# Eight products of a joint weight in float32 on the raw tiles, in place of 24 on split parts

## The chip, the core and the metric

The kernel runs on one core of one Trainium2 chip. The metric is the device time of one execution in microseconds. A core has a matrix engine (TensorE, PE in the profile, with its weight loads as PEld), a vector engine (VectorE, DVE), a scalar engine (ScalarE, ACT), GpSimd (POOL) and a sync engine (SyncE, SP) that issues most transfers. PE writes its products into PSUM, eight banks of 128 x 512 float32 values; the other engines read them from there. Each engine takes its instructions in order and waits for others by semaphores.

## The reference

One layer over 2048 positions of width 1024: a pooling branch and a gated recurrence, merged by gates and projected, and then a feed-forward part with a short convolution. What matters here is the pooling branch:

```python
mixed = jnp.einsum('bsgc,gcd->bsgd', pooled, pool_w).reshape(B, S, POOL_WIDTH)
return mixed * pool_scale
...
ya = pool_mixer(u_pool, pool_w[l], pool_scale[l]) @ w_pa[l]
...
merged = gates[:, :, 0] * ya + gates[:, :, 1] * yb
```

Two linear maps follow one another without anything between them: the mix of each group of 128 channels (pool_w, 4 groups of 128 x 128, with a scale for each channel), and w_pa (512 x 1024). The kernel multiplies the two weights with each other once, into a joint weight, and later applies that to the pooled channels.

## The kernel before

The 2048 positions are worked in blocks of 512, two blocks at a time (b0 = 0, then b0 = 2). For each pair come the input projection, the mixer with the recurrence, the branch projections, the output projection and the feed-forward part.

**Seven products for eight.** Each projection is written as a scheme of seven block products P1 to P7 (in the order P1, P6, P5, P7, P2, P4, P3 for the units of the input projection). A `Unit` has three PSUM banks, X, Z and V. P6 goes into Z, then P5 into V, then P7 into Z again. Between P6 and P7 DVE has to read Z out (`u2`, L1226 in the kernel before); between P7 and P4 it has to read it again (`u3`, L1230). So P7 can't start until `u2` is done. The trace calls both `u`.

**Split operands.** Nearly every product is made of three: each float32 operand is split into a high and a low part of type float32r, and high x high, high x low and low x high are added up in PSUM. A `Stream` prepares the weights: it loads a raw tile of 128 x 512 (`raw`, L198, on SP's queue, 8 buffers), ACT casts it to the high part (L232), DVE subtracts that from the raw tile (L233), and the pair is a tile `ops` (6 buffers). For some tiles POOL first adds two or more raw tiles (L461), and the sums are stored for the second pair of blocks (the `kw` tiles, L343).

**The order.** The program is written down once, with no loop on the chip. Each product of `mm` counts, and every six of them make a tick. A tick converts at most one weight (not more than `LOOKAHEAD` = 4 ahead of its use) and moves the waiting tasks on. The tasks are generators that wait some ticks between their steps: the recurrence of each head (`hgrn_task`, with small float32 products `pl`, `pk`, `pv`, `po` and `pt` on PE and long chains on DVE), the pooling sums, and the preparation of later weights. A scheduler then orders the instructions of each engine by a timeline of its own. So how many products a place has also decides where everything after it lands.

**The joint weight.** In the first pair of blocks, `both` runs after each of eight units of the input projection (from the unit `u`, 0 on). Its operand `pw` is the pooling weight: ACT scales it by the channel scale in four pieces (L409), and it is then split like every weight. The other operand, `cw`, is an eighth of w_pa, also split. Three products into a bank (`cw0` to `cw7` in the program, `cw` in the trace), a copy by ACT (L973) and two stores (`wb`, L979) finish one. The joint weight is read back as `pa` weights much later.

In the trace the units are fr (the recurrence's forget gate and query), gr (gates), ur (pooling channels) and pa; the number that follows in the program (gr0_2 is the gate unit 2 of the first pair) is left out there. All products made through `mm` show as L149.

Of the kernel before, what the change touches and what calls it, by code (L numbers as in the profile page):

```python
# [11 lines left out]
F32 = mybir.dt.float32  # L12
F32R = mybir.dt.float32r
U8 = mybir.dt.uint8
AF = mybir.ActivationFunctionType
# [3 lines left out]
P = 128  # L19
# [58 lines left out]
LOOKAHEAD = 4  # L78
# [4 lines left out]
def tile_trunk(  # L83
# [16 lines left out]
    pe, act, dve, pool, sp = nc.tensor, nc.scalar, nc.vector, nc.gpsimd, nc.sync  # L100
# [4 lines left out]
    opsp = ctx.enter_context(tc.tile_pool(name="opsp", bufs=N_OPS))  # L105
# [4 lines left out]
    def slot(name, cols=TB, dt=F32):  # L110
        return slots.tile([P, cols], dt, tag="s", name=name, padded_shape=[P, 528])
# [25 lines left out]
    def tick():  # L137
        stream.advance(1)
        for t in list(tasks):
            t.wait -= 1  # L140
            if t.wait <= 0 and t.live:
                t.step()
# [5 lines left out]
    def mm(*args, **kw):  # L148
        count[1] = pe.matmul(*args, **kw)  # L149
        count[0] += 1  # L150
        if count[0] % MM_PER_TICK == 0:
            tick()
# [16 lines left out]
    class Stream:  # L169
# [47 lines left out]
        def convert(self):  # L217
            j = len(self.tiles)
            key, fn, raws = self.ops[j]
            while any(r.tile is None for r in raws):  # L220
                self.load()
            for r in raws:
                r.add()
            store_kept()
            v = fn(f"w{j}")
            t = opsp.tile([P, 2, 512], F32R, tag="ops", name=f"ops{j}")
            n = int(np.prod(v.shape[1:]))
            hi, lo = t[:, 0, :n], t[:, 1, :n]
            if len(v.shape) == 3:
                hi = hi.rearrange("p (a b) -> p a b", a=v.shape[1])  # L230
                lo = lo.rearrange("p (a b) -> p a b", a=v.shape[1])
            self.mark = act.copy(hi, v)  # L232
            low = self.low = dve.tensor_tensor(lo, v, f32(hi), ALU.subtract)  # L233
            if j in self.pins:
                for ins, other in zip((self.mark, low), self.pins[j]):
                    behind(ins, other)
            self.tiles.append((key, t))
            self.load_ahead()
# [43 lines left out]
    stream = Stream()  # L282
# [57 lines left out]
    def store_kept():  # L340
        while keeping:
            d, t, later = keeping.pop(0)
            ins = sp.dma_start(d, t)  # L343
            if later:
                behind(ins, stream.low)

    def plan_one(key, src):
        r = stream.raw(src)
        stream.op(key, lambda nm, r=r: r.tile, [r])
# [51 lines left out]
            fn, raws = unit[p]()  # L401
            stream.op(key, fn, raws)

    def scaled_pool(r):
        def fn(nm):
            t = slot(f"{nm}p")
            for g in range(4):
                c = slice(g * P, (g + 1) * P)
                act.activation(t[:, c], r.tile[:, c], AF.Copy, scale=col(o_ps + g))  # L409
            return t  # L410
        return fn

    def plan_mixer(b0):
        plan_io(b0)
        for n, (kind, i) in enumerate(PROJ):
            if not b0 and (kind, i) == ("u", 0):
                r = stream.raw(pool_wt)
                stream.op("pw", scaled_pool(r), [r])
            plan_unit("in", w_in_t, kind, i, ORDER, b0)
            if not b0 and 0 <= n - CW_AT < 8:  # L420
                g, c = divmod(n - CW_AT, 2)
                plan_one("cw", w_pa[g][:, c * 512 : c * 512 + 512])
        for d in range(2):
            unit = weights_of_unit([(lambda d=d, q=q: w_both.get((d, q))) for q in range(4)])
            for p in ORDER:
                fn, raws = unit[p]()
                stream.op("pa", fn, raws)
        for i in range(8):
            plan_one("pb", w_pb_t[i // 2][:, i % 2 * 512 : i % 2 * 512 + 512])
        plan_rows("wo", w_o, R_OUT, KD // 2)  # L430
# [158 lines left out]
    o_n1, o_n2, o_bg, o_ps, o_lb, o_hg, o_cb, o_cw = offs  # L589
# [8 lines left out]
    def col(o):  # L598
        return cols[:, o : o + 1]
# [361 lines left out]
    def both(n, w_mix):  # L961
        g, c = divmod(n, 2)
        w = stream.get("cw")
        m = slice(g * P, (g + 1) * P)
        ps = bank(f"cw{n}")
        before = count[1]
        mm(ps, w_mix[:, 0, m], w[:, 0], start=True, stop=False)
        behind(count[1], before)
        mm(ps, w_mix[:, 0, m], w[:, 1], start=False, stop=False)
        mm(ps, w_mix[:, 1, m], w[:, 0], start=False, stop=True)  # L970
        stream.used(1)
        t = slot(f"cw{n}")
        act.copy(t, ps)  # L973
        q = 2 * c + g // 2
        for d in range(2):
            if (d, q) not in w_both:
                w_both[d, q] = dram.tile([P, 512], F32, tag=f"wb{d}{q}", name=f"wb{d}{q}")
            to = w_both[d, q].rearrange("p (e j m) -> p e j m", e=2, j=2)[:, :, g % 2]
            sp.dma_start(to, t[:, d * 256 : d * 256 + 256].rearrange("p (e m) -> p e m", e=2))  # L979
# [1016 lines left out]
```

## Time and profile before

| what | us |
|---|---|
| median of three runs (2512.33 to 2514.47) | 2512.68 |
| the profiled execution | 2511.63 |
| its span | 2509.9 |
| PE busy in the span | 2494.3 |
| DVE busy | 1997.0 |
| ACT busy | 1205.3 |
| POOL busy | 807.5 |
| first and last product of `cw` start at | 166.6 and 353.9 |

A line of a group gives the line of the code, the engine and operation, the output and inputs by the program's names, the shapes and the count, and then the busy time and the mean of one in ns. A line of a timeline begins with its start and its length in us; in brackets stands how long the engine was idle before it, and who released it. The chain of waits is read the same way, but each piece there is only the time that it adds to the chain. PE's products overlap, so the distance from start to start tells more than a product's own length. A float32 product shows in the trace as two records. "PEclk" is the share of TensorE's full clock that was granted.

### The profile page before, as it was taken

How to read it: one execution, taken by the hardware profiler on the slowest of the kernel's cores; microseconds unless marked ns; L12 is line 12 of the kernel's file. 1: busy time of each engine (PE TensorE's matmuls, PEld its weight loads, DVE VectorE, ACT ScalarE, POOL GpSimd, SP SyncE). 2: the span in 40 equal slices, each digit the busy share in tenths (PEclk: the TensorE clock that was granted, in tenths of full speed). 3: DMA queues.
4: the chain of work that ended last, by engine and by line, in shares of the span. 5: the costliest groups of instructions: out<-in, count | busy, mean ns of one | idle time of the engine just before them, and what ended most of it. 6: DMA issues, size and time to landing. Idle time of an engine off the chain costs nothing.

```text
span 2509.9 us, 35658 instructions
## 1 busy us (share of the span) xinstructions
PE 2494.3 (99%) x11436; PEld 2043.5 (81%) x11436; DVE 1997.0 (80%) x3519; ACT 1205.3 (48%) x2273; POOL 807.5 (32%) x1139
## 2 busy tenths in 40 slices
PE   9999999999999999999999999999999999999998
PEld 7887888888888888888888888887888888888887
DVE  7789778998998778885586777689979887778755
ACT  6534444434555445554554344443355555445534
POOL 4343354502354334451330201223033433325410
PEclk9999999999999999999999999999999999999999
DMA  8888788588898889897444343447444544447852
GB/s 272 270 206 231 233 219 258 203 243 249 203 260 230 231 226 241 265 363 246 126 148 151 117 130 107 139 147 255 130 150 122 154 149 139 150 135 247 320 165 100
DMA packets 257691, 497.68 MB, mean 198 GB/s; under 512 B 26912, under 2 KB 47520, under 8 KB 257184
## 3 DMA queue, kind: packets, MB, share of 16 engines
q1 hardware_dynamic: 189872, 317.53, 40.2%
q0 software_dynamic: 42656, 112.74, 17.8%
q10 hardware_dynamic: 24976, 65.13, 7.6%
q8 instruction: 90, 1.47, 0.2%
q14 instruction: 97, 0.79, 0.1%
HBM read 383.63 MB, written 189.27 MB: 228 GB/s over the span
## 4 chain that ended last, share of the span: by engine, by line
PE 90%; DVE 4%; ACT 1%; POOL 1%; DMA 1%; issue 1%; ACTq 0%; SPq 0%; POOLq 0%; DVEq 0%
PE dn_P L149 16%; PE up_Z L149 15%; PE up_V L149 10%; PE up_X L149 10%; PE wo_P L149 6%; PE gr_Z L149 4%; PE pb L149 4%; PE gr_V L149 3%; PE gr_X L149 3%; PE io_Z L149 3%; PE fr_Z L149 2%; PE io_V L149 2%; PE pl L1053 2%; PE ur_Z L149 1%; PE fr_V L149 1%; PE fr_X L149 1%
## 5 line engine op out<-in xcount | busy, mean ns | idle before, releaser
L232 ACT CAST ops<-raw 128x512 fp32r<-128x512 f32 x800 | 494.0, 621 | 860.9 <-PE dn_P L149 177.7
L233 DVE TENSOR_TENSOR ops<-raw,ops 128x512 fp32r<-128x512 f32 x800 | 596.6, 749 | 208.9 <-ACT ops L232 201.6
L1730 DVE SCALAR_TENSOR_TENSOR e<-h,cols,e 128x512 f32<-128x512 f32 x176 | 143.1, 817 | 31.3 <-ACT e L1728 26.7
L1728 ACT ACTIVATE e<-h,cols 128x512 f32<-128x512 f32 x176 | 142.2, 814 | 25.2 <-DVE h L1186 18.4
L988 POOL DMA_DIRECT2D g_P<-dg_P x154 | 84.3, 549 | 161.5 <-PE dn_P L149 110.9
L1733 DVE SCALAR_TENSOR_TENSOR e<-h,cols,e 128x512 f32<-128x512 f32 x176 | 133.8, 769 | 2.5
L1299 POOL TENSOR_TENSOR gf_P<-e,e 128x512 f32<-128x512 f32 x44 | 61.1, 1390 | 150.2 <-DVE e L1739 92.6
L461 POOL TENSOR_TENSOR raw<-raw,raw 128x512 f32<-128x512 f32 x36 | 50.4, 1401 | 167.5 <-DVE ops L233 115.6
L1299 POOL TENSOR_TENSOR gf_P<-gf_P,e 128x512 f32<-128x512 f32 x44 | 59.2, 1345 | 71.8 <-DVE e L1739 71.3
L1723 POOL COPY h<-h 128x2 f32<-128x2 f32 x88 | 40.5, 472 | 117.4 <-DVE h L1185 110.4
L1439 POOL TENSOR_TENSOR q<-q,qs 128x512 f32<-128x512 f32 x16 | 22.4, 1400 | 160.5 <-ACT qs L1438 160.5
L1725 POOL COPY hist<-h 128x2 f32<-128x2 f32 x88 | 36.2, 411 | 117.6 <-DVE h L1186 115.8
L1737 ACT ACTIVATE e<-e 128x512 f32<-128x512 f32 x88 | 55.6, 632 | 38.2 <-DVE e L1733 38.0
L1186 DVE TENSOR_TENSOR h<-up_u,up_V 128x512 f32<-128x512 f32 x88 | 60.0, 682 | 10.3 <-PE up_V L149 9.8
L1274 DVE TENSOR_TENSOR x<-x,wo_P 128x512 f32<-128x512 f32 x88 | 55.7, 679 | 7.7 <-PE wo_P L149 7.2
L1472 ACT ACTIVATE gt<-gt,cols 128x512 f32<-128x512 f32 x48 | 34.8, 726 | 56.0 <-DVE gt L1186 40.7
L1274 DVE TENSOR_TENSOR ac<-ac,dn_P 128x512 f32<-128x512 f32 x72 | 47.1, 680 | 16.5 <-PE dn_P L149 16.2
L1038 POOL COPY qm<-q 128x64 f32<-128x64 f32 x64 | 26.6, 448 | 103.4 <-DMA gd<-gt 20.0
L1753 POOL DMA_DIRECT2D dg_P<-gf_P x88 | 50.6, 576 | 8.1 <-POOL gf_P L1299 7.4
L1224 ACT COPY up_e<-up_X 128x512 f32<-128x512 f32 x44 | 25.8, 586 | 57.2 <-PE up_X L149 52.1
L1723 POOL COPY h<-hist 128x2 f32<-128x2 f32 x88 | 44.1, 508 | 27.7 <-DVE m_T42l L675 27.7
L1053 PE MATMUL pl<-qm,k 128*128 128x192 f32 x256 | 50.6, 328 | 0.0
(1337 smaller groups left out, 8077.7 us busy)
## 6 DMA issues: line engine op xcount, KB each, us to landing
g_P<-dg_P POOLq DMA_DIRECT2D x154, 256.0 KB, 6.1
raw<-in_w_up_t SPq DMA_DIRECT2D x132, 256.0 KB, 3.4
raw<-in_w_in_t SPq DMA_DIRECT2D x98, 256.0 KB, 3.6
dg_P<-gf_P POOLq DMA_DIRECT2D x88, 256.0 KB, 4.0
dg_P<-e SPq DMA_DIRECT2D x66, 256.0 KB, 3.4
raw<-in_w_dn SPq DMA_DIRECT2D x66, 256.0 KB, 4.2
x<-in_x SPq DMA_DIRECT2D x64, 256.0 KB, 5.0
gd<-gt ACTq DMA_DIRECT2D x64, 256.0 KB, 3.7
```

Of the source, the lines that this page charges most:

```text
L149: count[1] = pe.matmul(*args, **kw)
L232: self.mark = act.copy(hi, v)
L233: low = self.low = dve.tensor_tensor(lo, v, f32(hi), ALU.subtract)
L988: eng.dma_start(t, d)
L1053: ins = pe.matmul(pa_[:, c * 192 : c * 192 + 192], ks[:, (i + c) * P : (i + c + 1) * P], mv[:, c].rearrange("p s x -> p (s x)"), start=Tru ...
L1186: return dve.tensor_tensor(dst, t, ps, ALU.add if how == "add" else ALU.subtract)
L1274: dve.tensor_tensor(t, t, ps[j], ALU.add if sg > 0 else ALU.subtract)
L1299: pin(eng.tensor_tensor(t, x0, x1, op))
L1723: pool.tensor_copy(h[:, 0:2], hist[:, mt] if hf == 0 else hs[s, 0][:, TB : TB + 2])
L1728: in_turn(act.activation(t, h[:, 2:], AF.Identity, bias=col(o_cb + mt), scale=col(o_cw + 4 * MF + mt)))
L1730: in_turn(second(dve.scalar_tensor_tensor(t, h[:, 1 : 1 + TB], col(o_cw + 2 * MF + mt), t, ALU.mult, ALU.add)))
L1733: dve.scalar_tensor_tensor(t, h[:, 0:TB], col(o_cw + mt), t, ALU.mult, ALU.add)
```

## The change

`cw` is no longer split: `both` takes the raw float32 tile of w_pa as the moving operand. `pw` is no longer split either: the scaled pooling weight is written as float32 into the tile that held the pair. So each place has one float32 product where it had three of float32r. The stream's list keeps its entries, so a `cw` still takes its turn in a tick, without work. The raw tile of `cw` is now held until it has been used: its `last` is set six entries later, and loads that would need its buffer come later on SP's queue.

```diff
@@ convert
             for r in raws:
                 r.add()
+            if key == "cw":
+                self.tiles.append((key, raws[0].tile))
+                self.load_ahead()
+                return
+            if key == "pw":
+                t = opsp.tile([P, 2, 512], F32, tag="ops", name=f"ops{j}")
+                for g in range(4):
+                    c = slice(g * P, (g + 1) * P)
+                    act.activation(t[:, 0, c], raws[0].tile[:, c], AF.Copy,
+                                   scale=col(o_ps + g))
+                self.tiles.append((key, t[:, 0]))
+                self.load_ahead()
+                return
             store_kept()
             v = fn(f"w{j}")
@@ plan_mixer
-                stream.op("pw", scaled_pool(r), [r])
+                stream.op("pw", None, [r])
...
-                plan_one("cw", w_pa[g][:, c * 512 : c * 512 + 512])
+                r = stream.raw(w_pa[g][:, c * 512 : c * 512 + 512])
+                stream.op("cw", None, [r])
+                r.last += LOOKAHEAD + 2
@@ both
-        mm(ps, w_mix[:, 0, m], w[:, 0], start=True, stop=False)
+        mm(ps, w_mix[:, m], w, start=True, stop=True)
         behind(count[1], before)
-        mm(ps, w_mix[:, 0, m], w[:, 1], start=False, stop=False)
-        mm(ps, w_mix[:, 1, m], w[:, 0], start=False, stop=True)
```

The line numbers of the changed kernel are 13 higher in the stream, and 4 or 6 higher from the tasks on (`u2` is L1230 there, the `pl` products of two levels are L1057).

What it does to the order is shown at three places. The first is PE at the end of the unit gr0_1, where the third joint product (`cw2`) stands, and the first product of gr0_2. Before:

```order
L149 MATMUL gr0_1_V_2327<-x1_B223h_1118,ops65_2336 128x512
L1053 MATMUL pl0_1_4_2_2509<-qm0_1_4_2_2428,k0_1_2237 128x192 x2
L149 MATMUL cw2_2517<-ops66_2364,ops42_1546 128x512 x3
L149 MATMUL gr0_2_X_2525<-x0_f0h_255,ops67_2408 128x512
L149 MATMUL gr0_2_X_2525<-x0_f0l_256,ops67_2408 128x512
```

and now:

```order
L149 MATMUL gr0_1_V_2314<-x1_B223h_1118,ops65_2321 128x512
L149 MATMUL cw2_2492<-raw59_2003,ops42_1540 128x512
L149 MATMUL gr0_2_X_2498<-x0_f0h_255,ops67_2378 128x512
L149 MATMUL gr0_2_X_2498<-x0_f0l_256,ops67_2378 128x512
L149 MATMUL gr0_2_X_2498<-x0_f0h_255,ops67_2378 128x512
L1057 MATMUL pl0_1_4_2_2511<-qm0_1_4_2_2426,k0_1_2229 128x192 x2
```

Three products became one that reads the raw tile, and the recurrence's `pl` moved behind the first three products of the next unit.

The second place is DVE ahead of `u2` of gr0_2 (`at`, `qm`, `k`, `q` and `f` are tiles of the recurrence, its first index is the block). Before:

```order
L1074 TENSOR_TENSOR k1_1_2297<-k1_1_2297,f1_1_2218 128x32x12
L1070 TENSOR_TENSOR q1_1_2091<-q1_1_2091,f1_1_2218 128x8x16
L1042 TENSOR_TENSOR qm1_1_16_0_2605<-qm1_1_16_0_2605,f1_1_2218 128x2x64
L1042 TENSOR_TENSOR qm1_1_16_2_2611<-qm1_1_16_2_2611,f1_1_2218 128x2x64
L1064 COPY_PREDICATED at1_1_2300<-m33_1072,pl1_1_4_2_2588 128x16x8
L1044 TENSOR_TENSOR q1_1_2091<-qm1_1_16_0_2605,f1_1_2218 128x4x32
L1061 COPY_PREDICATED at0_1_2240<-m16_968,pl0_1_16_0_2617 128x8x16
L1044 TENSOR_TENSOR q1_1_2091<-qm1_1_16_2_2611,f1_1_2218 128x4x32
L1073 TENSOR_TENSOR f1_1_2218<-f1_1_2218 128x8
L1064 COPY_PREDICATED at1_1_2300<-m32_1028,pl1_1_4_2_2588 128x16x8
L1226 TENSOR_TENSOR gr0_2_u2_2623<-gr0_2_e1_2574,gr0_2_Z_2576 128x512
```

and now:

```order
L1078 TENSOR_TENSOR k1_1_2288<-k1_1_2288,f1_1_2205 128x32x12
L1068 COPY_PREDICATED at1_1_2291<-m33_1072,pl1_1_4_2_2576 128x16x8
L1230 TENSOR_TENSOR gr0_2_u2_2582<-gr0_2_e1_2547,gr0_2_Z_2549 128x512
L1043 TENSOR_TENSOR qm1_1_16_0_2603<-q1_1_2077,f1_1_2205 128x2x2x16
L1043 TENSOR_TENSOR qm1_1_16_2_2609<-q1_1_2077,f1_1_2205 128x2x2x16
L1068 COPY_PREDICATED at1_1_2291<-m32_1028,pl1_1_4_2_2576 128x16x8
L246 TENSOR_TENSOR ops73_2590<-raw63_2265,ops73_2590 128x512
L1074 TENSOR_TENSOR q1_1_2077<-q1_1_2077,f1_1_2205 128x8x16
L1046 TENSOR_TENSOR qm1_1_16_0_2603<-qm1_1_16_0_2603,f1_1_2205 128x2x64
L1046 TENSOR_TENSOR qm1_1_16_2_2609<-qm1_1_16_2_2609,f1_1_2205 128x2x64
L1065 COPY_PREDICATED at0_1_2232<-m16_968,pl0_1_16_0_2615 128x8x16
```

`u2` moved ahead of the `qm1` pair, of the products with `f1` and of the copies from `pl0_1_16_0`.

The third place is SP, the loads of raw tiles (L198 in both) around the first joint product; raw57 and raw58 belong to the gate unit 1, raw59 is the third eighth of w_pa. Before:

```order
L198 DMA raw56_1794<-in_w_in_t 128x512
L198 DMA raw57_1830<-in_w_in_t 128x512
L343 DMA kwfq1ins3_1958<-raw50_1484 128x512
L343 DMA kwfq1ins2_1896<-w52s2_1893 128x512
L343 DMA kwfq1ins1_1927<-raw51_1516 128x512
L198 DMA raw58_1962<-in_w_in_t 128x512
L979 DMA wb00_1949<-cw0_1947 256x1x128
L979 DMA wb10_1951<-cw0_1947 256x1x128
L198 DMA raw59_1964<-in_w_pa 128x512
```

and now:

```order
L198 DMA raw56_1791<-in_w_in_t 128x512
L356 DMA kwfq1ins3_1950<-raw50_1484 128x512
L356 DMA kwfq1ins1_1919<-raw51_1516 128x512
L356 DMA kwfq1ins2_1888<-w52s2_1885 128x512
L198 DMA raw57_1999<-in_w_in_t 128x512
L198 DMA raw58_2001<-in_w_in_t 128x512
L198 DMA raw59_2003<-in_w_pa 128x512
L983 DMA wb00_1939<-cw0_1937 256x1x128
L983 DMA wb10_1941<-cw0_1937 256x1x128
```

raw57 moved behind three stores, and raw59, which waited for a subtraction on DVE before, moved ahead of the two `wb` stores and now waits for PE, since it takes the buffer that the first eighth held.

More of the change, by code (lines that the diff above doesn't have):

```diff
@@ L402, in plan_unit @@
             stream.op(key, fn, raws)
[L404 to L411, printed above, removed]
     def plan_mixer(b0):
```

## The prediction, made before the changed kernel was run

> **What bounds the kernel now.** I read the page first: the span, the busy shares and the chain that ended last.
>
> ```profile
> span 2509.9 us, 35658 instructions
> PE 2494.3 (99%) x11436; PEld 2043.5 (81%) x11436; DVE 1997.0 (80%) x3519; ACT 1205.3 (48%) x2273; POOL 807.5 (32%) x1139
> PE 90%; DVE 4%; ACT 1%; POOL 1%; DMA 1%; issue 1%; ACTq 0%; SPq 0%; POOLq 0%; DVEq 0%
> ```
>
> TensorE (PE) is the bound. Only two things can move the time: the length of a product on PE, and the moments in which PE stands still. The profiled execution took 2511.63 us, 1.73 us outside its span; the median of the three runs is 2512.68, 1.05 more. I make the sum against 2511.63 and add 1.05 at the end.
>
> The second view is the list of what PE waited for, between 160 and 480 us, the stretch in which the changed products lie (columns: total us, times, longest).
>
> ```profile
> PE gr_Z L149 <- DVE gr_u L1226: 2.3, 1, 2.3
> PE pl L1093 <- ACT q L1010: 0.5, 1, 0.5
> PE pa_Z L149 <- DVE pa_u L1226: 0.4, 1, 0.4
> PE pa_Z L149 <- DVE pa_u L1230: 0.3, 1, 0.3
> ```
>
> One wait of 2.3 us outweighs the others together. It is in the gate unit gr_2. Its P7 writes into the Z bank that VectorE (DVE) must first read out (`u2`, L1226). In the timeline of PE:
>
> ```profile
> 230.41 0.40 PE L149 MATMUL gr_V<-x_T13l,ops 128*128 128x512 f32 x1
> 230.64 0.39 PE L149 MATMUL gr_V<-x_T13h,ops 128*128 128x512 f32 x1
> 233.34 0.50 PE L149 MATMUL gr_Z<-x_T30h,ops 128*128 128x512 f32 x1 [2.31 <-DVE gr_u L1226]
> ```
>
> Products of 512 columns start 0.23 us apart, so P7 could have started at 230.87. The third view is the busy time by stretches. The long rows name PE, PEld, DVE, ACT and POOL in turn; the short ones were asked for PE's L149 alone. The granted clock stands ahead of the DMA share.
>
> ```profile
> 210.50:230.90 20.40, 20.40 (x100) 16.99 (x98) 20.37 (x61) 8.43 (x18) 9.94 (x12) 1.00 0.90 249
> 230.90:233.30 2.40, 0.13 (x1) 0.00 (x0) 2.40 (x12) 0.62 (x1) 0.00 (x0) 1.00 0.86 100
> ...
> 234.00:236.00 2.00, 1.65 (x5) 0.70 1.09 253
> 236.00:238.00 2.00, 1.53 (x4) 0.50 1.13 227
> 238.00:240.00 2.00, 1.68 (x6) 0.95 0.69 244
> ```
>
> DVE had no gap in the 20 us before (20.37 of 20.40 busy): it was late because its queue was long. And right behind PE's gap the clock was halved: (1-0.70)x2 + (1-0.50)x2 + (1-0.95)x2 = 1.7 us of PE's work were lost. The gap and the slow stretch together cost 2.3 + 1.7 = 4.0 us.
>
> **The change part by part.** *The product itself.* Three split products become one in float32. Before, in the timeline of PE:
>
> ```profile
> 166.59 0.86 PE L149 MATMUL cw<-ops,ops 128*128 128x512 f32 x3
> 167.29 0.39 PE L149 MATMUL fr_X<-x_f0h,ops 128*128 128x512 f32 x1
> ```
>
> Start to start the three took 0.70 us. No float32 product of 512 columns is in the trace. The nearest are those of 192 columns (`pl`, L1053) and of 128 (`pk`); each shows as two records, so x4 are two products and x8 are four.
>
> ```profile
> 143.38 0.81 PE L1053 MATMUL pl<-qm,k 128*128 128x192 f32 x4
> 143.89 0.53 PE L149 MATMUL ur_X<-x_f2h,ops 128*128 128x512 f32 x1
> 144.26 0.81 PE L1053 MATMUL pl<-qm,k 128*128 128x192 f32 x4
> ...
> 169.38 1.03 PE L1127 MATMUL pk<-ident,k 128*128 128x128 f32 x8
> 170.17 0.48 PE L149 MATMUL fr_X<-x_f3h,ops 128*128 128x512 f32 x1
> 170.48 0.39 PE L149 MATMUL fr_X<-x_f3l,ops 128*128 128x512 f32 x1
> ```
>
> I take each group with the 512-column product behind it, whose start is drawn too early, and take its 0.23 off. 192 columns: (144.26-143.38-0.23)/2 = 0.325 us. 128 columns: (170.48-169.38-0.23)/4 = 0.217 us. Both are 1.7 ns a column, so 512 columns come to 0.865 us. That is 0.165 more than the three, eight times: **+1.3 us**, all on PE, which nothing hides. The bounds: 0.325 (no dearer than at 192 columns) would be -3.0 us in all, four passes of 0.23 each would be 0.92 and +1.8 us. I take 0.865, since two widths lie on one line.
>
> *The conversions.* Nine pairs go (eight parts of w_pa and the pooling weight), each a cast on ScalarE (ACT) and a subtraction on DVE:
>
> ```profile
> L232 ACT CAST ops<-raw 128x512 fp32r<-128x512 f32 x800 | 494.0, 621 | 860.9 <-PE dn_P L149 177.7
> L233 DVE TENSOR_TENSOR ops<-raw,ops 128x512 fp32r<-128x512 f32 x800 | 596.6, 749 | 208.9 <-ACT ops L232 201.6
> ```
>
> 9 x 0.62 = 5.6 us of ACT and 9 x 0.75 = 6.7 us of DVE. Neither is the bound, so this is worth nothing by itself; cover is PE's stream. It is worth something where DVE's queue decides, at gr_2. The pooling weight's four scalings stay.
>
> *The order around it.* A tick comes every six products, and each place loses two, so the tasks' instructions move later against the unit products. That moves work behind gr_2's `u2` on DVE (the second pair of rows above, in the part on the change). What goes from ahead of it, by the chain of waits, where DVE's pieces follow one another:
>
> ```profile
> 210.60 0.60 DVE ops L233
> ...
> 228.80 0.26 DVE qm L1039 x2
> ...
> 231.00 0.20 DVE q L1070
> ...
> 231.61 0.20 DVE at L1064
> ...
> 232.69 0.61 DVE gr_u L1226
> ```
>
> The subtraction for `cw2` at 210.60 is gone (0.60). The pair `qm1` at 228.80 stands behind (0.26), and so does all from 231.00 up to `u2` (1.69) except the copy at 231.61 (0.20), which stays ahead: 0.60 + 0.26 + 1.49 = 2.35 us. So `u2` starts at 230.34 and ends, 0.68 long as an instruction, at 231.02. PE would be ready for P7 at 230.87 plus three dearer products (`cw0` to `cw2`, 0.5) = 231.4. The gap closes with 0.4 us to spare, and with it the cause of the slow stretch: **-4.0 us**. The bounds: nothing, if other waits of DVE take its place, and -4.0; I take the whole, as DVE's queue was unbroken.
>
> Next late is gr_1. There two groups of `pl` and `pt` go from ahead of P7 to behind it, and PE comes 1.35 us earlier:
>
> ```profile
> 202.05 0.76 DVE L233 TENSOR_TENSOR ops<-raw,ops 128x512 fp32r<-128x512 f32 x1
> ...
> 203.07 0.68 DVE L1226 TENSOR_TENSOR gr_u<-gr_e,gr_Z 128x512 f32<-128x512 f32 x1
> ...
> 203.44 1.16 PE L1093 MATMUL pl<-q,k 128*128 128x128 f32 x8
> ...
> 204.79 0.48 PE L149 MATMUL gr_Z<-x_T30h,ops 128*128 128x512 f32 x1
> ```
>
> P7 now wants to start at 203.44 + 2 x 0.165 = 203.8. `u2` ended at 203.75, and one subtraction (0.69) ahead of it is gone: 203.1. Nothing is lost, with 0.7 us to spare.
>
> *The loads.* The raw tile of w_pa is now held until PE has read it. Up to two loads a unit go behind stores and `w_pa`'s own load, which then waits for PE; behind it in SyncE's (SP's) queue stand the `wb` stores, a `kw` store and the next loads, which the adds on GpSimd (POOL) wait for. The loads of the unit gr_2 and their first use:
>
> ```profile
> 180.76 3.12 SPq L198 DMA_DIRECT2D raw<-in_w_in_t  x2
> ...
> 191.47 0.32 SPq L343 DMA_DIRECT2D kwg1ins<-w60s  x1
> ...
> 211.28 2.65 POOL L461 TENSOR_TENSOR raw<-raw,raw 128x512 f32<-128x512 f32 x2 [5.62 <-DMA kwg1ins<-raw]
> ```
>
> 30 us lie between. The second of them goes behind four more instructions of SP, to after the store of `w60s` at 191.47; a slip of 8 us is hidden and costs nothing. If the cover were gone, PE would lose what is late, one to one.
>
> **The sum.** +1.3 - 4.0 = -2.7 us. 2511.63 - 2.7 = 2508.9, and with the 1.05 by which the runs' median lies higher, 2510.0.
>
> **A rule beside the trace.** The row: the clock was at 1.00 in the 2.40 us of the gap and at 0.50 by 236. The Trainium skill, TensorE: Matmul & The Clock Gate, Part 1 (the HAM clock gate), says that PE goes back to half clock after at least one idle window of about 3.4 us. By it 2.3 us of idling are too short, and the slow stretch would have another cause and could stay; the trace speaks for the gap as cause, since the slow stretch starts within 2 us of it.
>
> **The rivals.**
> 1. The gap closes but the slow stretch stays, wherever it then falls: +1.3 - 2.3 = -1.0, 2511.7. For it: a slow stretch was not seen behind the other waits, none of which was over 0.5 us here, so one case is all there is. Against it: its place. This is what the page's rule above would make of it.
> 2. The change doesn't reach the wait: DVE comes to `u2` as late as before, because what was moved is replaced by waits for PE's `pl` products, which also moved later. Then +1.3 alone, 2514.0.
> 3. Slower: the wait goes to gr_1. If DVE reaches `u2` there 3.0 us later than worked out (the 0.7 to spare and a gap of 2.3), PE has a gap as long as the old one and again a slow stretch, 4.0 us, while gr_2's stays as it is: +1.3 + 4.0 = +5.3, 2518.0. For it: P7 comes 1.35 us earlier there. Against it: one subtraction less ahead. Below 3 us it doesn't decide.
> 4. Faster: all four waits of the list go (3.5 us) with the slow stretch (1.7), and the float32 product costs no more than the three did: -5.2, 2507.5. For it: DVE has 6.7 us less to do. Against it: the last two waits are in `pa`, where nothing moved, and the two widths' common price.
>
> **How the numbers follow.** A measurement of this kernel tells about 0.2% (5 us) from no change. Forecast 0.54, rival 1 0.10, rival 2 0.12, rival 3 0.12, rival 4 0.12. The time is the forecast's, 2510.0. The range must leave out no more than 0.2: it takes in rivals 1 and 2 and most of 4 and leaves out rival 3, with 1 us for small waits on each side, 2506.5 to 2515.1. Faster by over 0.2%: rival 4, 0.12. Slower: rival 3, 0.12. Within: the rest, 0.76.
>
> **What would show it.** In the changed kernel's profile: `cw` as two records a product, 0.86 us start to start for the pair; 9 casts and 9 subtractions fewer; no wait of PE for `gr_u` over 0.5 us; the clock at 1.00 from 200 to 300 us; SP's loads later by less than 10 us and no wait of POOL for them. I am wrong if a wait of over 2 us appears at another Z bank between 160 and 400 us, if the slow stretch is there without a gap, or if a `cw` pair takes more than 0.95 us.

## The result and the profile after

| | median, us | lowest to highest | runs |
|---|---|---|---|
| kernel before, measured beside it | 2513.57 | 2510.28 to 2517.34 | 8 |
| changed kernel | 2505.28 | 2504.59 to 2507.14 | 8 |

The ratio is 0.9967, with a 95% interval of 0.9956 to 0.9978: 8.3 us less, 0.33%. The forecast was 2510.0, with a range from 2506.5 to 2515.1, so the time lies 1.2 us below the range. The direction was right; the size was three times the forecast's 2.7 us.

The profiled execution took 2505.04 us, 6.6 less than the one of before. Its page, in the lines that answer to those shown of before:

```profile
span 2503.3 us, 35640 instructions
PE 2490.4 (99%) x11428; PEld 2039.1 (81%) x11428; DVE 1977.8 (79%) x3510; ACT 1201.1 (48%) x2264; POOL 805.1 (32%) x1139
PE 97%; DVE 1%; ACT 0%; DMA 0%; issue 0%; POOL 0%; SPq 0%; ACTq 0%; DVEq 0%
L245 ACT CAST ops<-raw 128x512 fp32r<-128x512 f32 x792 | 489.3, 621 | 826.4 <-PE dn_P L149 176.6
L246 DVE TENSOR_TENSOR ops<-raw,ops 128x512 fp32r<-128x512 f32 x792 | 590.4, 749 | 202.8 <-ACT ops L245 198.4
```

The chain that ended last now runs on PE for 97% of its length, where it was 90%, and on DVE for 1%, where it was 4%. That is not the gain itself: 3% of the span are 75 us, and 6.6 were won. The chain counts all that led up to a wait, and the waits themselves stand in the next list. DVE has nine instructions fewer (3510 for 3519) and so has ACT (2264 for 2273): the nine pairs of conversions. Eight of them stood in the two groups shown; the pooling weight's pair had another input and its own row.

What PE waited for between 160 and 480 us, the whole list:

```profile
PE pa_Z L149 <- DVE pa_u L1230: 0.4, 1, 0.4
```

The wait of 2.3 us for `gr_u` is gone, and so is that of 0.5 for `q`. The busy time by stretches, the same stretches as before (PE, PEld, DVE, ACT, POOL, granted clock, DMA):

```profile
210.50:230.90 20.40, 20.40 (x99) 17.16 (x98) 19.83 (x71) 8.61 (x20) 8.00 (x12) 1.00 0.94 234
230.90:233.30 2.40, 2.40 (x12) 1.93 (x11) 2.02 (x7) 0.62 (x1) 0.44 (x1) 1.00 1.11 213
234.00:236.00 2.00, 2.00 (x13) 1.84 (x11) 1.75 (x4) 0.21 (x1) 1.92 (x3) 1.00 0.41 151
236.00:238.00 2.00, 2.00 (x16) 1.47 (x14) 1.71 (x5) 0.51 (x1) 0.78 (x1) 1.00 0.66 250
```

PE is busy all through, and the clock stays at 1.00. DVE has some idle time again (19.83 us busy of 20.40, where it was 20.37). In its timeline `u2` of gr_2 comes here:

```profile
227.53 0.68 DVE L1230 TENSOR_TENSOR gr_u<-gr_e,gr_Z 128x512 f32<-128x512 f32 x1
```

and in PE's, P7 follows P5 without a wait; ahead of them the first `cw`:

```profile
166.85 1.02 PE L149 MATMUL cw<-raw,ops 128*128 128x512 f32 x2
167.30 0.79 PE L149 MATMUL fr_X<-x_f0h,ops 128*128 128x512 f32 x1
167.94 0.39 PE L149 MATMUL fr_X<-x_f0l,ops 128*128 128x512 f32 x1
...
230.99 0.40 PE L149 MATMUL gr_V<-x_T13h,ops 128*128 128x512 f32 x1
231.23 0.39 PE L149 MATMUL gr_Z<-x_T30h,ops 128*128 128x512 f32 x1
```

The `cw` pair starts at 166.85, and the product after the next at 167.94. Taking off one product of 0.23 leaves 0.86 us for the float32 product.

To see where the 6.6 us came from I set each product of PE beside the same product of before, and took how much earlier it starts (medians over nine neighbours):

| place in the profile of before, us | changed kernel earlier by |
|---|---|
| 225 | 0.1 |
| 243 to 249 (behind gr_2's P7) | 3.8 to 4.6, as other products moved past |
| 364 (all eight float32 products paid) | 3.0 |
| 392 | 3.8 |
| 600 | 4.6 |
| 1250 | 5.3 |
| 1275 | 6.1 |
| 2480 | 6.6 |

Up to 364 us the forecast holds (2.7 forecast, 3.0 measured). The other 3.6 us of the profiled difference came later, in steps of under 1 us: 0.8 at 385 us, where PE had waited 0.5 for `q`, 0.8 at 1260 us, where it had waited 0.7 for `x_xs` at the start of the second pair of blocks, and the rest in smaller pieces. And the medians lie 8.3 us apart, 1.7 more than the two profiles: that is a matter of the kernel before, of which the last experiments speak.

### The profile page after: what moved, and what is told of

It reads as the page before. It is cut to its first block, busy times and chain, and to the rows that moved or that the text cites. A ratio compares the mean times of both kernels' runs of the same rounds, so it can differ in the third digit from the quotient of the medians.

```text
span 2503.3 us, 35640 instructions
## 1 busy us (share of the span) xinstructions
PE 2490.4 (99%) x11428; PEld 2039.1 (81%) x11428; DVE 1977.8 (79%) x3510; ACT 1201.1 (48%) x2264; POOL 805.1 (32%) x1139
## 4 chain that ended last, share of the span: by engine, by line
PE 97%; DVE 1%; ACT 0%; DMA 0%; issue 0%; POOL 0%; SPq 0%; ACTq 0%; DVEq 0%
PE dn_P L149 17%; PE up_Z L149 15%; PE up_X L149 10%; PE up_V L149 10%; PE wo_P L149 6%; PE gr_Z L149 5%; PE gr_X L149 4%; PE gr_V L149 4%; PE pb L149 4%; PE io_Z L149 3%; PE fr_Z L149 3%; PE fr_X L149 2%; PE fr_V L149 2%; PE io_V L149 2%; PE pl L1057 2%; PE ur_Z L149 1%
## 5 line engine op out<-in xcount | busy, mean ns | idle before, releaser
L246 DVE TENSOR_TENSOR ops<-raw,ops 128x512 fp32r<-128x512 f32 x792 | 590.4, 749 | 202.8 <-ACT ops L245 198.4
L1057 PE MATMUL pl<-qm,k 128*128 128x192 f32 x256 | 50.0, 325 | 0.0
```

The costliest lines, as they stand in the source:

```text
L1057: ins = pe.matmul(pa_[:, c * 192 : c * 192 + 192], ks[:, (i + c) * P : (i + c + 1) * P], mv[:, c].rearrange("p s x -> p (s x)"), start=Tru ...
```

## The experiments

### The order alone

The kernel before with its 24 split products, of which only the first of each place counts for a tick, as in the changed kernel.

```diff
-        mm(ps, w_mix[:, 0, m], w[:, 1], start=False, stop=False)
-        mm(ps, w_mix[:, 1, m], w[:, 0], start=False, stop=True)
+        pe.matmul(ps, w_mix[:, 0, m], w[:, 1], start=False, stop=False)
+        count[1] = pe.matmul(ps, w_mix[:, 1, m], w[:, 0], start=False, stop=True)
```

> The kernel before with all its 24 split products and all conversions, but the second and third product of each place don't count for the ticks, so that the tasks' instructions land as in the changed kernel. Theory A (the gain is the order: the tick shift takes VectorE's work from ahead of u2 at gr_2 and so the gap of 2.3 us and the half clock behind it): the gap is closed, no dearer product is paid, so 1.3 us below the changed kernel's median of 2505.3, about 2504. Theory B (the gain is the relief of ScalarE and VectorE by nine conversions): nothing changes, about 2513.6, the gap at gr_2 still 2 us or more.

Measured: 2507.48 us (2505.61 to 2509.29, 10 runs) against 2514.77 of the kernel before beside it (19 runs), ratio 0.9974 [0.9965, 0.9983]. In PE's timeline two waits for `u2` are left:

```profile
205.73 0.50 PE L149 MATMUL gr_Z<-x_T30h,ops 128*128 128x512 f32 x1 [1.45 <-DVE gr_u L1226]
...
233.45 0.50 PE L149 MATMUL gr_Z<-x_T30h,ops 128*128 128x512 f32 x1 [0.30 <-DVE gr_u L1226]
```

At gr_2 the wait shrinks from 2.3 to 0.3 us, and a new one of 1.45 appears at gr_1. That is the place the third rival named, with a smaller price. So the order alone doesn't close the waits, it moves most of one to the unit before. In DVE's timeline `u2` of gr_2 comes no earlier than before:

```profile
232.72 0.67 DVE L1226 TENSOR_TENSOR gr_u<-gr_e,gr_Z 128x512 f32<-128x512 f32 x1
```

It ends at 233.4, and at 233.3 in the kernel before. The wait there is short because PE comes 2.1 us later, for the most part by the 1.45 at gr_1 and by 0.8 that it lost at 184 us to a wait of which the last experiments speak. DVE was held by those 0.8 as well, so the order brought `u2` forward by some 0.7 us; the forecast had counted 1.75 for it. Theory B falls, since the gap is no longer 2 us, and Theory A misses by 3.5 us. But no stretch of half clock follows the 1.45 us: from 200 to 300 us the granted clock is 1.00.

```profile
200.00:300.00 100.00, 98.25 (x513) 82.34 (x512) 81.88 (x205) 49.17 (x108) 37.67 (x43) 1.00 0.80 227
```

### The conversions alone

The changed kernel, with each float32 product counted as three, so that the ticks fall as before.

```diff
         mm(ps, w_mix[:, m], w, start=True, stop=True)
         behind(count[1], before)
+        for _ in range(2):
+            count[0] += 1
+            if count[0] % MM_PER_TICK == 0:
+                tick()
```

> The changed kernel, but each float32 product counts as three for the ticks, so that the order of the tasks stays as before; conversions are gone and the product is the float32 one. Theory A: the gap at gr_2 stays, smaller by the one subtraction that is gone (0.6 us) and by PE's 0.5 us of dearer products, so 1.2 us or so, perhaps with the half clock: 2511 to 2514. Theory B: as the changed kernel, about 2505.3, no gap.

Measured: 2507.06 us (2505.99 to 2509.59, 8 runs), ratio 0.9974 [0.9964, 0.9984]. PE's waits between 160 and 480 us:

```profile
PE fr_Z L149 <- DVE fr_u L1234: 0.5, 1, 0.5
PE pa_Z L149 <- DVE pa_u L1234: 0.4, 1, 0.4
PE pa_Z L149 <- DVE pa_u L1238: 0.3, 1, 0.3
```

No wait for `gr_u` is left, at gr_1 or gr_2. In DVE's timeline:

```profile
229.11 0.67 DVE L1234 TENSOR_TENSOR gr_u<-gr_e,gr_Z 128x512 f32<-128x512 f32 x1
```

`u2` of gr_2 ends at 229.8, 3.5 us earlier than before and 1.2 ahead of P7 (231.03). Theory A falls. With the old count of ticks, what is left of the change suffices: the missing conversions, the loads that moved, and one product in place of three. The forecast had credited one missing subtraction (0.60 us) ahead of it. This kernel has the changed kernel's loads, though; none of the kernels moves the loads without the rest, so what part they have in the 3.5 us is open.

### The order with the conversions done for nothing

The changed kernel, in which the eight casts and subtractions of w_pa are made and their result is not used.

```diff
             if key == "cw":
+                t = opsp.tile([P, 2, 512], F32R, tag="ops", name=f"ops{j}")
+                self.mark = act.copy(t[:, 0], raws[0].tile)
+                self.low = dve.tensor_tensor(t[:, 1], raws[0].tile, f32(t[:, 0]), ALU.subtract)
                 self.tiles.append((key, raws[0].tile))
```

> The changed kernel, with the eight casts and subtractions of w_pa done all the same into a tile that nobody reads. Theory A: within 1 us of the changed kernel, 2505 to 2506, no gap at gr_2, since u2 has 3.0 us to spare there. Theory B: most of the gain goes, about 2512.

Measured: 2506.29 us (2505.06 to 2507.53, 6 runs), ratio 0.9969 [0.9957, 0.9981]. No wait for `gr_u` and no half clock here either, so Theory B falls; in PE's timeline one wait for `fr_u` has come:

```profile
179.68 0.50 PE L149 MATMUL fr_Z<-x_T30h,ops 128*128 128x512 f32 x1 [0.98 <-DVE fr_u L1233]
```

In DVE's timeline that `fr_u` stood 4.93 us for the landing of a store of the joint weight (`wb`). The median is 1.0 us over the changed kernel's 2505.28, which the overlapping intervals of the two ratios don't tell from nothing.

Together with the first two experiments: the half clock goes by either half of the change, and so does the gap at gr_2, but for 0.3 us, while with the order alone 1.45 us of wait turn up at gr_1. The two halves don't add up, since both remove the same thing. Here too the loads are those of the changed kernel; the order alone, with the old loads, did less for `u2`.

### The shift of the ticks up to the eighth place only

The changed kernel, which from the eighth place on has its 16 missing counts given back, so that the ticks of all later stages fall as before.

```diff
                 if n - CW_AT == 7:
                     stream.used(1)
+                    for _ in range(16):
+                        count[0] += 1
+                        if count[0] % MM_PER_TICK == 0:
+                            tick()
```

> The changed kernel, with the 16 counts of the ticks given back right after the eighth place, so that from 360 us on the ticks fall as they did before. The profiles put 3.8 us of the gain before 420 us and 2.8 us behind it. Theory C (the later part comes from the changed phase of the ticks): the later 2.8 us go, about 2508. Theory D (the later part comes from elsewhere, for example from transfers that run earlier or from chance): about 2505.3.

Measured: 2506.76 us (2506.46 to 2507.37, 6 runs), ratio 0.997 [0.9958, 0.9981]. The median is 1.5 us over the changed kernel's; the shortest of these runs is longer than seven of the eight of the changed kernel, though the intervals of the ratios overlap. The profiles say the same more clearly: set beside the profile of before as above, this kernel is 4.2 us earlier at 392 us and still 4.2 at 2480, while the changed kernel goes from 3.8 to 6.6. So the shifted ticks of the later stages brought 1.5 (by the medians) to 2.8 us (by two profiles of the changed kernel and one of this) of the 3.6 that the forecast lacks; nothing in it reached beyond the joint weight's own stages. That is Theory C, in the profiles with its full size.

### The gap put back

The changed kernel with five, and then six, further reads of gr_2's Z bank by DVE ahead of `u2`, whose results nothing uses.

```diff
+                    for _ in range(5):
+                        more.append(dve.tensor_tensor(z, t["e1"], bk["Z"], ALU.subtract))
...
+                ins = dve.tensor_tensor(self.tmp("u2"), t["e1"], bk["Z"], ALU.subtract)
+                if more:
+                    behind(ins, more[-1])
```

> The changed kernel with five further reads of gr_2's bank Z on VectorE ahead of the subtraction u2 (into a tile that nothing reads), so that u2 ends later and TensorE waits again at gr_2's product P7, at about 2 us; everything else of the change stays, and the result is the reference's. Theory G (the gap and the half clock behind it are worth what the profile of before shows: 2.3 us and 1.7 us): a gap of about 2 us, perhaps with a half-clock stretch behind it, and a time 2.0 to 3.7 us over the changed kernel's 2505.3, so 2507 to 2509, with a spread of the runs as small as the changed kernel's (2.5 us). Theory H (a gap with half clock costs more in most runs than in the profiled one, and is what spreads the times of before over 8 us): the half clock shows, the median is 5 to 8 us over the changed kernel's, 2510 to 2513, and the runs spread over 6 us or more.

> The same with six further reads, so that the wait at gr_2's P7 comes back at about 3.4 us, over the 2.3 us that it had before. Theory G: 3.4 us for the gap and 1.7 us for the slow stretch, so about 2510.4, with a small spread. Theory H: 2512 to 2515 and a spread of 6 us or more. If neither a half-clock stretch nor a spread comes back behind a gap this long, then the half clock does not come from the gap, and the step of the forecast that tied it to the gap falls.

Measured: 2506.51 us (2506.41 to 2508.03, 5 runs) with five, ratio to before 0.9962 [0.995, 0.9975], and 2509.86 us (2508.22 to 2511.09, 8 runs) with six, 0.9975 [0.9965, 0.9985]. The stretches of the first:

```profile
232.00:234.00 2.00, 1.06 (x4) 0.84 (x5) 2.00 (x7) 0.07 (x1) 0.00 (x0) 0.87 0.73 197
234.00:236.00 2.00, 2.00 (x6) 1.61 (x5) 2.00 (x6) 0.00 (x0) 1.89 (x2) 0.50 0.04 7
236.00:238.00 2.00, 2.00 (x8) 1.55 (x8) 1.97 (x4) 0.00 (x0) 2.00 (x2) 0.78 0.35 131
```

and of the second:

```profile
234.00:236.00 2.00, 1.03 (x4) 0.90 (x5) 2.00 (x6) 0.00 (x0) 2.00 (x3) 0.95 0.03 11
236.00:238.00 2.00, 2.00 (x6) 1.52 (x6) 2.00 (x1) 0.00 (x0) 2.00 (x3) 0.50 0.87 164
238.00:240.00 2.00, 2.00 (x8) 1.56 (x7) 1.97 (x8) 0.00 (x0) 0.70 (x1) 0.69 0.99 156
```

With five reads PE waited 1.9 us, with six 3.3, and behind both the clock halves. What is lost is (1-0.87)x2 + (1-0.50)x2 + (1-0.78)x2 = 1.7 us, and (1-0.95)x2 + (1-0.50)x2 + (1-0.69)x2 = 1.7 us, as it was before: a stretch of 3.4 us at half clock each time, wherever it begins. So the half clock at gr_2 comes from the gap, which settles the first rival.

Theory G (the gap and 1.7 us, as the profile shows) gives 5.0 us for the long gap; measured are 4.6 in the medians and 5.3 between the profiled runs. Theory H falls: with the gap and the half clock back, the eight runs spread over 2.9 us, not over 6. For the short gap, where it gives 3.6, the profiled run (2507.72) lies 2.7 us over the changed kernel's, and the median of all five only 1.2 us over; three of the five lie between 2506.41 and 2506.51. That these three had no half clock would fit, but they were not profiled.

One caution goes for all medians from here on. These runs, and those of the gap filled and of each product twice, were taken on another chip than the experiments above. The kernel before had a median of 2516.27 us beside them, 2514.77 beside those above and 2513.57 beside the changed kernel, which was not run there. A difference of 1 or 2 us to the changed kernel's median is therefore uncertain, and the stretches and timelines above count for more.

### The gap filled

The kernel before, with nine of the twelve matmuls of gr_2's P5 done once more ahead of the real ones, for nothing.

```diff
+            if p == "P5" and self.name == "gr0_2":
+                for k in range(3):
...
             for k in range(n):
                 wh, wl = w[:, 0, k * P : (k + 1) * P], w[:, 1, k * P : (k + 1) * P]
```

The nine matmuls themselves stand where the dots are.

> The kernel before, in which nine of the twelve matmuls of gr_2's P5 (the three ahead of u2's end) are done twice, first for nothing: TensorE then works on through the 2.3 us in which it waited for u2 at P7, and nothing else is changed. Nine matmuls of 0.23 us are 2.07 us, so P7 starts where it did or up to 0.3 us earlier; the wait shrinks to about 0.3 us. If the half clock comes from the gap, it does not show. Theory G: 1.7 us less than before in the profile, and in the median too, about 2512.5. Theory H: more than that in the median, 4 to 7 us less than before (2507 to 2510), with a spread of at most 4 us in place of 8. If the half clock stays at 235 us with no gap ahead of it, it has another cause than the gap (the first rival), and the median stays within 1 us of before.

Measured: 2510.47 us (2509.0 to 2516.14, 11 runs), ratio 0.9979 [0.997, 0.9988]. PE's wait at gr_2, and the stretches behind:

```profile
PE gr_Z L149 <- DVE gr_u L1236: 0.2, 1, 0.2
```

```profile
234.00:236.00 2.00, 2.00 (x10) 1.79 (x11) 1.97 (x8) 0.40 (x1) 0.00 (x0) 1.00 1.08 229
236.00:238.00 2.00, 2.00 (x12) 1.74 (x11) 1.93 (x7) 0.00 (x0) 0.00 (x0) 1.00 1.12 226
```

No gap, no half clock. The profiled run took 2509.93, 1.7 us less than the profiled run of before: Theory G's number to the tenth. That it fits so well is partly luck: PE gained 1.6 us between 225 and 249 us, as the theory has it, but it had lost 0.6 before and gained 0.8 at 385 us, which the filling doesn't explain. But the median is 5.8 us under that of the kernel before beside it (2516.27, 24 runs), as Theory H wanted, which had just fallen. One run of 2516.14 shows that the filled kernel too can lose some 5 us. So something that the profile of before did not show was in most of the runs of before.

### Each product twice

```diff
         mm(ps, w_mix[:, m], w, start=True, stop=True)
         behind(count[1], before)
+        count[1] = pe.matmul(ps, w_mix[:, m], w, start=True, stop=True)
```

> The changed kernel with each of the eight float32 products done twice into the same bank: prices the float32 product on the path. At the 0.865 us of the forecast 8 x 0.865 = 6.9 us more than the changed kernel, 2512.2. If a float32 product costs no more than the three that it replaced (0.70 us, the fourth rival's condition), 5.6 us more, 2510.9. If part of it is hidden by waits, less than 5 us.

Measured: 2512.36 us (2511.13 to 2513.71, 11 runs), 7.1 us over the changed kernel, and 6.6 between the profiled runs (2511.59 and 2505.04): 0.885 and 0.82 us a product. Measured against the kernel before beside each (0.9986 and 0.9967), it would be 4.8 us, 0.6 a product; but that kernel's own median differs by 2.7 us between the two. PE's timeline decides. There the pair and its repetition start 0.86 us apart:

```profile
166.84 1.02 PE L149 MATMUL cw<-raw,ops 128*128 128x512 f32 x2
167.70 1.02 PE L975 MATMUL cw<-raw,ops 128*128 128x512 f32 x2
```

The forecast's 0.865, drawn from products of 192 and 128 columns, holds, and the float32 products did cost more than the three, against the condition of the fourth rival.

### The kernel before, profiled again

What was open: the runs of before, 56 in all over these measurements, have a median of 2514.8 us and go from 2509.6 to 2519.3. The profiled run, at 2511.63, is among the shortest. Three more profiles were taken, of the same kernel.

> The kernel before, unchanged, profiled anew. Its runs have spread from 2509.6 to 2519.3 us with medians of 2513 to 2516, while the profiled one took 2511.63 and is so one of its short ones. Theory J (the wait at gr_2 is longer in a usual run than in the profiled one, since VectorE comes to u2 later still, and the half-clock stretch with it): a profile of 2514 us or more shows a wait for gr_u of 4 us or more and two to four us more lost between 225 and 240 us, and equal progress of TensorE from there on. Theory K (another half-clock stretch or wait, which the profiled run happened not to have): the wait at gr_2 is 2 to 2.5 us as before, and the time is lost at another place, with a granted clock of 0.5 or a wait of over 1.5 us that the first profile doesn't have. Theory L (the start): it is lost in the first 30 us. A profile of under 2512.5 us tells nothing new.

> The same, once more: theory J a wait for gr_u of 4 us or more if the time is 2514 us or more, and nothing elsewhere; theory K a wait of 2 to 2.5 us there and a further loss of 2 to 5 us at another place; theory L a loss in the first 30 us.

> The same, a third time, to see whether a loss that the first two show falls at the same place each time (theory J: at gr_2 between 225 and 240 us, 2 to 5 us; theory K: at another place; theory L: in the first 30 us).

Measured: 2513.22, 2517.65 and 2512.24 us. PE's longest waits between 160 and 480 us in the second, the longest run:

```profile
PE gr_Z L149 <- DVE gr_u L1226: 2.3, 1, 2.3
PE fr_Z L149 <- DVE fr_u L1230: 2.3, 1, 2.3
PE pl L1093 <- ACT q L1010: 2.1, 2, 1.6
PE po L1154 <- DVE ss L1144: 0.6, 1, 0.6
```

and in the third:

```profile
PE gr_Z L149 <- DVE gr_u L1226: 2.3, 1, 2.3
PE po L1154 <- DVE ss L1144: 1.4, 2, 0.8
```

The wait at gr_2 is 2.3 us in all four profiles, so Theory J falls. Theory K holds: there are further waits, which the first profile had by luck hardly any of. Single waits of over 1.5 us, the size that the theory asked for, stand in the longest run alone. How much later PE is than in the first profile:

| profile of before, its time | 183 us | 188 us | 364 us | 376 us | 392 us | 1250 us | 1275 us |
|---|---|---|---|---|---|---|---|
| first repetition, 2513.22 | 0.0 | 1.5 | 1.6 | 1.5 | 2.5 | 2.5 | 1.6 |
| second, 2517.65 | 0.1 | 1.2 | 1.3 | 3.7 | 5.5 | 6.1 | 6.1 |
| third, 2512.24 | 0.0 | 2.2 | 2.3 | 2.2 | 1.4 | 1.5 | 0.6 |

Nothing is lost ahead of 183 us, so Theory L falls. The third repetition shows more: at 385 and at 1260 us it gains 0.8 and 0.9 us on the first profile. Those are two of the steps at which the changed kernel gained, and here nothing was changed.

Two of these places were followed back, and both hang on when a store lands. At 184 us PE waits for a DVE chain (`ss`) whose first piece waits for the store of `p`. DVE's timeline, first profile and third repetition:

```profile
181.12 0.35 DVE L1144 SCALAR_TENSOR_TENSOR ss<-st,f,pv 128x128 f32<-128x128 f32 x1 [2.27 <-DMA md<-p]
```

```profile
183.30 0.35 DVE L1144 SCALAR_TENSOR_TENSOR ss<-st,f,pv 128x128 f32<-128x128 f32 x1 [4.93 <-DMA md<-p]
```

The same store lands 2.2 us later, and PE is 2.2 us later behind it. At 372 us the wait in the second repetition goes back to ACT:

```profile
368.58 0.62 ACT L232 CAST ops<-raw 128x512 fp32r<-128x512 f32 x1 [6.51 <-DMA wb<-cw]
```

ACT stood 6.5 us ahead of this cast, DVE's subtraction stood behind it, then `fr_u`, and then PE. By the semaphores in the trace, ACT was held by its own next store, of `p`: that is counted on the semaphore of a store of the joint weight (`wb`) that SP had issued a few us earlier, and ACT's instruction waits until that one has landed. In the first profile ACT's store went 5.0 us after SP's (356.40 to 361.41), in the second repetition 10.8 us (357.32 to 368.16). The transfers' times to landing, first profile and second repetition:

```profile
wb<-cw SPq DMA_DIRECT2D x2, 128.0 KB, 7.0
```

```profile
wb<-cw SPq DMA_DIRECT2D x2, 128.0 KB, 11.2
```

In the changed kernel the loads of SP fall in another order, and with them which transfers share a semaphore: that store of `p` (358.92) follows a transfer issued 7.0 us earlier (351.96), not 5.0.

**A gap without half clock.** The wait for `fr_u` in the second repetition is as long as the one at gr_2, but the clock stays at 1.00 behind it. PE's timeline, and its busy time in two stretches of 3.41 us with the granted clock:

```profile
372.57 0.50 PE L149 MATMUL fr_Z<-x_T40h,ops 128*128 128x512 f32 x1 [2.27 <-DVE fr_u L1230]
```

```profile
368.31:371.72 3.41, 1.99 (x9) 1.00 0.89 338
371.72:375.13 3.41, 2.56 (x11) 1.00 0.94 307
```

So the length of a gap does not decide alone. Where the half clock begins gives a hint. In the first profile and in the first and third repetition another such stretch stands at the start, at 9.51, 7.65 and 8.13 us, and the one behind gr_2 begins 225.28, 228.69 and 228.69 us later: 66, 67 and 67 times 3.413 us, the length of a half-clock stretch. If the clock goes by fixed stretches of that length, a gap that falls across the border of two counts as two shorter ones. Counted from each profile's own half clock (with the order alone the only one is behind the last product):

| gap of PE, its start in us | idle in each stretch that it falls into | clock in the next |
|---|---|---|
| before, 2.31 at 231.03 | 0.34, 1.97 | 0.50 |
| before, second repetition, 2.31 at 232.26 | 2.31 | 0.50 |
| five further reads, 1.92 at 231.02 | 1.92 | 0.50 |
| six further reads, 3.32 at 231.65 | 0.75, 2.57 | 0.50 |
| before, second repetition, 2.27 at 370.30 | 1.42, 0.85 | 1.00 |
| order alone, 1.45 at 204.28 | 0.81, 0.64 | 1.00 |

In all 14 profiles, up to 5 us ahead of their end, the clock halves behind each stretch with 1.89 us or more of idling, behind one of the four with 1.76 to 1.83, and behind none with less. No run moved a gap within such a stretch and left the rest alone, so this is a reading of the figures, not a test.

### The changed kernel, profiled again

> The changed kernel, unchanged, profiled anew. Theory K (before, TensorE loses 1 to 6 us in most runs at waits that hang on when stores land, at 184, 372 and 385 us, and the change takes these away with the wait at gr_2): a time of 2504.5 to 2507.2 us, and none of the waits of TensorE for ss, fr_u or q between 160 and 480 us is over 1 us; VectorE's wait for the store of p ends by 181 us. If one of them is there with 1.5 us or more and the time is still under 2507.5, theory K does not explain what the changed kernel gained beyond the forecast.

Measured: 2504.76 us. PE's waits between 160 and 480 us, and DVE's wait for the store of `p`:

```profile
PE pa_Z L149 <- DVE pa_u L1230: 0.4, 1, 0.4
```

```profile
179.35 0.35 DVE L1148 SCALAR_TENSOR_TENSOR ss<-st,f,pv 128x128 f32<-128x128 f32 x1 [2.22 <-DMA md<-p]
```

None of the varying waits is there, and the store has landed early enough, as Theory K asked. The three further profiles of before were taken on the other chip and this one on that of the first experiments, so the chip is a rival. Against it, the runs of before spread over 8 us on either, and the late store shows on the first chip too, in the kernel with the order alone: there that wait of DVE still ended at 182.2 us, and PE was 0.8 us later behind it; in the one with the conversions alone it ended at 179.3. In one profile each, that points to the loads and conversions rather than the ticks. But in the kernel with each product twice, which has the changed kernel's loads, it ended at 183.4, so which part of the change does it stays open. So does why most runs of the kernel with the gap filled were as short as they were, though its transfers share semaphores as before.

## Why the prediction was right, and where not

**The float32 product** (+1.3 us): right. 0.86 us in the trace, 0.82 to 0.885 by doubling, 0.865 forecast.

**The conversions**: nine fewer, as forecast. "It is worth something where DVE's queue decides" was right, but only one subtraction was credited for it. With the loads that moved and the one product, it was enough to close the gap without the new order.

**`u2` at gr_2**: right that the gap closes, wrong in the size of the room. `u2` was to end at 231.02, 0.4 us ahead of P7; it ended at 228.2 (227.53 and 0.68 long), 3.0 us ahead of P7 at 231.23. The forecast moved single instructions within the old queue, and took everything ahead of gr_2 as it stood. In the experiments the order alone brings `u2` forward by some 0.7 us, where 1.75 were counted, and the rest of the change by 3.5, where 0.60 were counted; together they bring 5.1. So the gap closed with more room than forecast, and for another reason in the main. How the 3.5 divide between conversions, loads and the product was not taken apart.

**gr_1**: right. `u2` was to be 0.7 us early, and no wait came. `u2` ended at 202.63, 1.3 us ahead of P7. With the order alone 1.45 us of wait do come, where the forecast's terms without the subtraction and the dearer products give 0.3 (203.75 less 203.44), and with the conversions done for nothing none comes. So that the missing subtraction was needed there is not shown.

**Gap and slow stretch** (-4.0 us): right at this place. Putting a gap back brought 1.7 us of half clock with it twice, and filling it took 1.7 away. That the gap at gr_2 had the half clock behind it in each of four profiles is not a rule for every gap of its length, as the 2.27 us at 370 us show. As to the rule beside the trace: the Trainium skill, TensorE: Matmul & The Clock Gate, Part 1, has the clock fall after at least one idle window of about 3.4 us. Here gaps of 1.9 and 2.3 us were enough at gr_2, while one of 2.27 elsewhere and one of 1.45 were not, so as a lower limit for a gap the rule fails. Each half-clock stretch, though, was 3.4 us long, which agrees with the window that the page names.

**Loads**: the late ones cost PE nothing, as forecast. POOL's longest waits for `raw` were for DVE. But "no wait of POOL for them" did not hold: at 284.6 us POOL stood 7.3 us for a load, which the profile of before doesn't have; PE had no wait from it.

**The step that failed** is the end of the sum: "2511.63 - 2.7 = 2508.9, and with the 1.05 by which the runs' median lies higher, 2510.0", and with it "1 us for small waits on each side" in the range. It took everything outside gr_2 as it stood, and added the 1.05 to the changed kernel as if it belonged to any kernel. Two sizes were wrong in it. First, the waits elsewhere: 3.6 us of the profiled difference lie behind 364 us, 1.5 to 2.8 us of it by the shifted ticks there; the forecast had nothing for them. Two steps of it, 0.8 us each, may be chance, since the kernel before shows them too from one run to another. Second, the 1.05 itself: the changed kernel's median lies 0.24 over its profiled run, while that of before lies 1.9 over it in the runs beside the changed kernel, and 3.2 over all 56. That excess was no constant: the three further profiles show it as varying waits at 184, 372 and 385 us, and neither profile of the changed kernel has them. The fourth rival, with all listed waits gone, came nearest (2507.5), though its condition on the product's price was false. With the price as it is it would have said 2508.8, and the 3.5 us from there are waits that its list didn't hold. (The range's upper end, 2515.1, should be 2515.0 by its own terms.)

**What was to show it**: two records a product at 0.86 us, the conversions, no wait for `gr_u`, and the clock at 1.00 from 200 to 300 us were all seen; POOL's wait for a load was not to be there. None of the three signs of a wrong forecast appeared, and yet the time was outside the range: the signs all concerned the place of the change.

## What to carry to other kernels

Where the median of a kernel lies above its profiled run, or the runs spread by more than the term you are estimating, profile the kernel again before you forecast: one profile shows the waits of one run, and a change that relieves a loaded engine can take away those you haven't seen too. A gap on TensorE of about 2 us could cost nearly twice its length here, because a stretch at half clock followed six of the seven gaps of 1.9 us and more that stand behind the first 100 us of the profiles; read the granted clock behind each gap before you price it. When two parts of a change relieve the same queue, test each alone before you give either the credit, the loads that move with it too.

## What was not expected of the hardware

- A gap of 1.92 us on PE was followed by half clock, one of 2.27 in another place was not, and the loss behind gaps of 1.9, 2.3 and 3.3 us was the same 1.7 us. How much of a gap lay within one fixed stretch of 3.41 us fits all of these cases.
- The median time to landing of two 128 KB stores of the joint weight went from 7.0 to 11.2 us between two runs of the same kernel at the same place. Through a shared semaphore that held ACT for 6.5 us, though ACT needed nothing of what was stored.
